# A diffusion block on one core: the modulation product in unsplit float32, in four column groups

## The chip, the core and the metric

The kernel runs on one core of a Trainium2 chip. Its time is the device time of one execution in microseconds (us). Five engines run side by side, each through its own instructions in order: TensorE (PE in the profile; PEld is its weight load), VectorE (DVE), ScalarE (ACT), GpSimd (POOL) and SyncE (SP), whose queue issues nearly all transfers from memory (HBM) to the on-chip buffer. TensorE multiplies a stationary operand, held in its 128 x 128 array, by a moving operand of up to 512 columns, and writes into one of eight banks.

## The reference, cut to what matters

One layer over 256 latent tokens (x) and 256 context tokens (ctx) of width 2048, all in float32. Its first step is the modulation:

```
mod   = silu(c)     @ w_mod + b_mod      # shift, scale, gate of the mixer, then of the MLP
mod_c = silu(c_ctx) @ w_mod + b_mod
hc = rms_norm(ctx) * g * (1 + scale_c) + shift_c
h  = rms_norm(x)   * g * (1 + scale)   + shift
```

`w_mod` is 2048 x 12288. For the mixer both vectors need its first 4096 columns, a shift and a scale for each of the 2048 channels; these are the tensor `wm0` of the kernel, 64 tiles of 128 x 1024 (512 KB each). Then come the input projection `h @ w_in` (its first part, the values, for both token streams), a gated linear recurrence and a convolution, two output projections, and a squared-ReLU MLP. The rest of the layer isn't touched by the change.

## The kernel before

A float32 weight tile is loaded by SP into one of five `raw` buffers, split into a rounded part (`whi`, ACT, line 84) and a remainder (`wlo`, DVE, line 85), both in the format float32r, and multiplied part by part. `Stream` does this in the order of a list (`items`), up to `AHEAD` = 4 tiles ahead of the use. SP waits for a `raw` buffer until DVE has read it.

The stage that the change touches is the first one. It has eight column blocks c, each of 256 channels; a block has eight steps t, one `wm0` tile each. A tile holds two k blocks of 128 rows side by side, each 512 columns wide (256 of the scale, 256 of the shift). In a step, lines 490 and 491 multiply each k block twice, once by `whi` and once by `wlo`; the stationary operand `s4` has four columns, silu(c) and silu(c_ctx), each split in two. So a block is 32 matmuls into four rows of one bank. Then `modulate(c, ps)` runs spread over steps 1 to 3 of the next block: the four rows are copied (line 453), turned into columns by four transposes on PE (line 457), the halves are added and the bias and the gain worked in (lines 466 to 469), which gives `A` and `B` for two channel blocks. `turn` (line 747 and on) then transposes the normed x and ctx for these two channel blocks (eight transposes), applies `A` and `B` on ACT and splits the result into `h` (line 185).

Between the steps, at the places in `STEPS`, half a tile of the values is worked off (`values`, lines 852 to 854): 12 matmuls of 512 columns against a tile of `w_in` (`wi0`, one load and one split for two halves). So a block from c = 2 on has 32 + 24 matmuls of 512 columns, eight transposes of x and ctx, four of `row`, and nine tiles to load and to split.

`norms` loads x and ctx in 8 tiles, in turn with the first weight tiles, sums their squares on ACT and scales them on DVE. After the stage, the rest of the values, the query and the recurrence follow; their tiles (and those of `dots` and `gemv`, which work the other parts of `w_mod` on DVE) come through the same list. [...]

Of the kernel before, what the change touches and what calls it, by code (L numbers as in the profile page):

```python
# [15 lines left out]
P = 128  # L16
# [19 lines left out]
STEPS = [(c, t) for c in range(1, 8) for t in (4, 7)][1:]  # L36
# [12 lines left out]
class Stream:  # L49
# [11 lines left out]

    def add_gemv(self, ap, fn):
        self.items.append((ap, fn, False))

    def prepare(self):
# [4 lines left out]
        raw = kn.wp.tile([P, TW], F32, name="raw", tag="raw", bufs=5)  # L70
        self.dma = nc.sync.dma_start(raw, ap)
        if fn is not None:
            fn(raw)
            return
# [13 lines left out]
    def next(self, ahead=AHEAD):  # L88
        while len(self.ready) < ahead and self.done < len(self.items):
            self.prepare()  # L90
        while ahead > 1 and self.done < len(self.items) and self.items[self.done][1] is not None:
            self.prepare()
        return self.ready.popleft()


class Kernel:
# [190 lines left out]
    def run(self):  # L287
# [18 lines left out]

        cc = pack[:, 0:32]
# [4 lines left out]
        s4 = self.cp.tile([P, KT * 4], F32R, name="s4")  # L312
        s4v = s4.rearrange("p (k f) -> p f k", f=4)
        for i in range(2):
            self.split(sc[:, i * 16:(i + 1) * 16], s4v[:, 2 * i, :], s4v[:, 2 * i + 1, :])
# [23 lines left out]
        for c in range(8):  # L339
            for t in range(8):  # L340
                steps.append((c, t))
                st.add(a["wm0"][8 * c + t])
                if (c, t) in STEPS:
                    steps.append(None)
                    if n % 2 == 0:
                        st.add(a["wi0"][n // 2], paged=True)
                    n += 1
# [68 lines left out]

        def norms():
            ssq = self.cp.tile([P, 8], F32, name="ssq0")
            junk = self.page(F32, "junk")[:, :TW]
            with self.tc.issue_after(exp.ins):  # L420
                nc.scalar.activation(out=first, in_=self.eps, func=AF.Sqrt)
            for n in range(10):
                if n < 8:
                    i, tb, h = n // 4, n // 2 % 2, n % 2
                    nc.sync.dma_start(xt[i][2 * tb + h][:, :TW], a[("x", "ctx")[i]][tb * P:(tb + 1) * P, h * TW:(h + 1) * TW])
                if n > 1:
                    m = n - 2
                    nc.scalar.activation(out=junk, in_=xt[m // 4][m % 4][:, :TW], func=AF.Square, accum_out=ssq[:, m:m + 1])
                if n in (2, 5, 7):
                    yield  # L430
            nc.vector.tensor_reduce(r4, ssq.rearrange("p (t n) -> p t n", n=2), axis=mybir.AxisListType.X, op=ALU.add)
            self.rstd(r4, r4, 1.0 / D)
            for h in range(2):
                for n in range(4):
                    s = xt[n // 2][2 * (n % 2) + h][:, :TW]
                    nc.vector.tensor_scalar(out=s, in0=s, scalar1=r4[:, n:n + 1], scalar2=None, op0=ALU.mult)
                    yield
# [12 lines left out]
        def modulate(c, ps):  # L450

            row = self.small(512, "row")[0:4, :]
            nc.scalar.copy(out=row, in_=ps[0:4, :])
            yield
            pt = self.bank()
            for j in range(4):
                nc.tensor.transpose(out=pt[:, 4 * j:4 * j + 4], in_=row[:, j * P:(j + 1) * P], identity=v["ident"][0:4, 0:4])
            yield

            cols = self.small(16, "cols").rearrange("p (n b i f) -> p n i b f", n=2, b=2, i=2)  # L460
            nc.scalar.copy(out=cols.rearrange("p n i b f -> p n b i f"), in_=pt[:, :16].rearrange("p (n b i f) -> p n b i f", n=2, b=2, i=2))
            ks = slice(2 * c, 2 * c + 2)
            for n, dst in enumerate((Av, Bv)):
                bm = v["bmod"][:, (1 - n) * KT + 2 * c:(1 - n) * KT + 2 * c + 2]
                for i in range(2):
                    nc.vector.tensor_tensor(dst[:, i, ks], cols[:, n, i, :, 0], cols[:, n, i, :, 1], op=ALU.add)
                    nc.vector.tensor_tensor(dst[:, i, ks], dst[:, i, ks], bm, op=ALU.add)
                    if n == 0:
                        nc.vector.scalar_tensor_tensor(dst[:, i, ks], dst[:, i, ks], 1.0, v["g_pm"][:, ks], op0=ALU.add, op1=ALU.mult)
# [5 lines left out]
        for step in steps:  # L475
# [6 lines left out]
            next(normed, None)  # L482
            if t in (1, 2, 3):
                next(late, None)
            hi, lo = st.next()
            for k2 in range(2):
                k = 2 * t + k2
                s = slice(k2 * 512, (k2 + 1) * 512)
                w = s4[:, 4 * k:4 * k + 4]
                nc.tensor.matmul(ps[0:4, :], w, hi[:, s], start=(k == 0), stop=False)  # L490
                nc.tensor.matmul(ps[0:4, :], w, lo[:, s], start=False, stop=(k == KT - 1))  # L491
# [3 lines left out]
        next(values)  # L495
        for _ in late:
            pass
        masks = self.cp.tile([P, 7 * P], U8, name="masks")
# [269 lines left out]
    def warm(self):  # L768

        ps = self.bank()  # L770
        for _ in range(WARM):
# [361 lines left out]
```

## Time and profile before

| | us |
|---|---|
| median of three runs | 1707.87 |
| lowest, highest | 1705.53, 1710.20 |
| the profiled execution, and its span | 1710.28, 1708.5 |
| PE busy in the span | 1665.9 (98%) |
| DVE, ACT busy | 1207.6 (71%), 871.0 (51%) |

The profile records one execution. A matmul's length in it is modelled, from its start to its drained end, so neighbours overlap: what one costs is the distance from its start to the next one's. "Idle before" is the time an engine stood still ahead of a group, with the instruction that ended it. The granted clock is a share of 2.4 GHz, 0.50 being 1.2 GHz.

### The profile page before, as it was taken

What the parts mean: (1) busy time and instruction counts of PE and PEld (TensorE: products, weight loads), DVE (VectorE), ACT (ScalarE), POOL (GpSimd) and SP (SyncE); (2) the same over time, 40 slices, a digit from 0 to 9 for tenths busy, and PEclk for the clock granted to TensorE, in tenths of its full rate; (3) what the DMA queues carried; (4) which work ended last, traced back from release to release, by engine and by line L of the source; (5) the groups of instructions that cost most, each with busy time, mean ns of one, the idle gap of its engine ahead of it and who ended that gap; (6) DMA issues with size and microseconds to landing.
All of it is one profiled execution on the core that took longest, in us unless ns stands there. A gap on an engine that the chain in (4) does not pass through costs nothing.

```text
span 1708.5 us, 23461 instructions
## 1 busy us (share of the span) xinstructions
PE 1665.9 (98%) x8794; PEld 1396.2 (82%) x8794; DVE 1207.6 (71%) x1720; ACT 871.0 (51%) x1268; POOL 8.1 (0%) x18
## 2 busy tenths in 40 slices
PE   5999999999999999999999999999999999999997
PEld 1557887888888888888888899888888888888886
DVE  6887767777776999987897566555665665556555
ACT  8785333344445444564455466445553455345543
POOL 0000000000000000000000000000000000000000
PEclk8999999999999999999999999999999999999999
DMA  9887984433356677668887556666666666666553
GB/s 329 303 303 283 338 283 155 143 125 109 111 162 202 205 236 235 220 202 272 292 273 258 168 198 224 214 228 234 220 208 224 231 227 209 230 222 199 185 188 122
DMA packets 103346, 374.57 MB, mean 219 GB/s; under 512 B 11584, under 2 KB 11584, under 8 KB 103232
## 3 DMA queue, kind: packets, MB, share of 16 engines
q1 hardware_dynamic: 101952, 368.86, 65.0%
q0 software_dynamic: 1280, 4.21, 0.8%
q8 instruction: 69, 1.13, 0.3%
q14 instruction: 45, 0.37, 0.1%
HBM read 370.93 MB, written 2.10 MB: 218 GB/s over the span
## 4 chain that ended last, share of the span: by engine, by line
PE 88%; DVE 4%; DMA 3%; ACT 3%; issue 2%; SPq 0%; DVEq 0%; ACTq 0%
PE bank L200 27%; PE bank L202 14%; PE bank L208 8%; PE bank L209 8%; PE bank L207 8%; PE bank L192 4%; PE bank L190 4%; PE bank L191 4%; DMA raw<-wm 2%; PE bank L910 2%; DVE wlo L85 2%; PE bank L852 1%; PE bank L854 1%; PE bank L853 1%; ACT turned L764 1%
## 5 line engine op out<-in xcount | busy, mean ns | idle before, releaser
L85 DVE TENSOR_TENSOR wlo<-raw,whi 128x1024 fp32r<-128x1024 f32 x547 | 665.5, 1223 | 329.4 <-ACT whi L84 322.9
L84 ACT ACTIVATE whi<-raw 128x1024 fp32r<-128x1024 f32 x547 | 575.6, 1059 | 573.6 <-PE bank L200 204.2
L200 PE MATMUL bank<-h,whi 128*128 128x512 f32 x2176 | 548.3, 394 | 0.0
L200 PEld LDWEIGHTS bank<-h,whi 128*128 128x128 f32 x2176 | 392.7, 189 | 70.6
L202 PEld LDWEIGHTS bank<-h,wlo 128*128 128x128 f32 x2176 | 296.7, 190 | 22.6 <-DVE wlo L85 1.3
L202 PE MATMUL bank<-h,wlo 128*128 128x256 f32 x2176 | 303.6, 282 | 0.5 <-DVE wlo L85 0.4
L207 PE MATMUL bank<-whi,hidh 128*128 128x512 f32 x500 | 194.6, 389 | 0.0
L208 PE MATMUL bank<-wlo,hidh 128*128 128x512 f32 x500 | 194.6, 389 | 0.0
L209 PE MATMUL bank<-whi,hidl 128*128 128x512 f32 x500 | 194.5, 389 | 0.0
L190 PE MATMUL bank<-h,whi 128*128 128x512 f32 (+1 forms) x384 | 140.7, 367 | 1.8 <-ACT whi L84 1.0
L191 PE MATMUL bank<-h,whi 128*128 128x512 f32 (+1 forms) x384 | 136.0, 355 | 0.0
L192 PE MATMUL bank<-h,wlo 128*128 128x512 f32 (+1 forms) x384 | 135.8, 355 | 0.0
L209 PEld LDWEIGHTS bank<-whi,hidl 128*128 128x128 f32 x500 | 93.8, 188 | 19.5
L207 PEld LDWEIGHTS bank<-whi,hidh 128*128 128x128 f32 x500 | 93.9, 188 | 19.4
L208 PEld LDWEIGHTS bank<-wlo,hidh 128*128 128x128 f32 x500 | 93.9, 188 | 19.3
L784 DVE SCALAR_TENSOR_TENSOR gacc<-raw,silu_c,gacc 128x1024 f32<-128x1024 f32 x60 | 76.9, 1282 | 44.3 <-DMA raw<-wm 44.3
L795 DVE SCALAR_TENSOR_TENSOR raw<-raw,silu_row 128x1024 f32<-128x1024 f32 x64 | 77.5, 1221 | 22.9 <-DMA raw<-wmt 22.8
L190 PEld LDWEIGHTS bank<-h,whi 128*128 128x128 f32 x384 | 72.7, 189 | 10.6 <-ACT whi L84 1.2
L192 PEld LDWEIGHTS bank<-h,wlo 128*128 128x128 f32 x384 | 72.3, 189 | 10.5 <-DVE wlo L85 0.3
L191 PEld LDWEIGHTS bank<-h,whi 128*128 128x128 f32 x384 | 72.8, 190 | 8.7 <-DVE h L185 0.3
L490 PE MATMUL bank<-whi,s 128*4 128x512 f32 x128 | 54.2, 423 | 16.6 <-ACT whi L84 16.6
L491 PE MATMUL bank<-wlo,s 128*4 128x512 f32 x128 | 53.8, 420 | 8.4 <-DVE wlo L85 7.9
(206 smaller groups left out, 1514.3 us busy)
## 6 DMA issues: line engine op xcount, KB each, us to landing
raw<-w SPq DMA_DIRECT2D x256, 512.0 KB, 4.2
raw<-wi SPq DMA_DIRECT2D x176, 512.0 KB, 4.2
raw<-wm SPq DMA_DIRECT2D x128, 512.0 KB, 4.6
raw<-wmt SPq DMA_DIRECT2D x64, 512.0 KB, 4.3
raw<-wo SPq DMA_DIRECT2D x32, 512.0 KB, 4.7
raw<-who SPq DMA_DIRECT2D x16, 512.0 KB, 4.4
raw<-wpw SPq DMA_DIRECT2D x16, 512.0 KB, 4.9
x<-x SPq DMA_DIRECT2D x4, 512.0 KB, 7.0
```

The source lines that it names most:

```text
L84: nc.scalar.activation(out=hi, in_=raw, func=AF.Copy)
L85: kn.los.append(nc.vector.tensor_tensor(lo, raw, hi.bitcast(F32), op=ALU.subtract))
L190: nc.tensor.matmul(out, w[0], x[0], start=first, stop=False)
L191: nc.tensor.matmul(out, w[0], x[1], start=False, stop=False)
L192: nc.tensor.matmul(out, w[1], x[0], start=False, stop=last)
L200: nc.tensor.matmul(bank, w[0][:, cut(i)], x(k)[2], start=(k == 0), stop=False)
L202: nc.tensor.matmul(bank[:, T:], w[1][:, cut(i)], x(k)[0], start=False, stop=(k == nk - 1))
L207: nc.tensor.matmul(out, x[0], w[0], start=first, stop=False)
L208: nc.tensor.matmul(out, x[0], w[1], start=False, stop=False)
L209: nc.tensor.matmul(out, x[1], w[0], start=False, stop=last)
L784: nc.vector.scalar_tensor_tensor(acc, raw, s, acc, op0=ALU.mult, op1=ALU.add)
L795: nc.vector.scalar_tensor_tensor(raw, raw, 1.0, self.srow, op0=ALU.mult, op1=ALU.mult, accum_out=self.dot[:, 32 * j + b:32 * j + b + 1])
```

## The change

The 64 `wm0` tiles are no longer split. `add_whole` loads them as they are, the odd steps' tiles into pages of a second pool, up to seven tiles ahead. The stationary operand `s32` holds 32 columns for each k block in plain float32, two of them silu(c) and silu(c_ctx), 30 of them zero. One matmul of line 503 takes the place of two: k block k is written to the 32 rows from 32 * (k % 4) on, that is, through column group k % 4 of the array. A block is 16 matmuls, four to each group. `modulate` copies all 128 rows, transposes 128 x 128 four times (line 470), and one reduction on DVE adds the four groups; fewer, wider instructions make `A` and `B`. x is loaded first, then ctx in turn with weight tiles; x and ctx are normed apart. PE does 32 matmuls of ones ahead of the first step and eight after each of the first four steps. The half tiles of the values go to steps 5 and 7 (before: 4 and 7), and their tiles are split into the ordinary `whi` and `wlo` buffers.

On PE before, around the transposes of x and ctx in the block c = 2 (L490 and L491 are the products with `whi` and `wlo`, L747 the transposes):

```order
L491 MATMUL bank_561<-wlo_534,s4_85 4x512
L490 MATMUL bank_561<-whi_533,s4_85 4x512
L491 MATMUL bank_561<-wlo_534,s4_85 4x512
L490 MATMUL bank_561<-whi_545,s4_85 4x512
L491 MATMUL bank_561<-wlo_546,s4_85 4x512
L490 MATMUL bank_561<-whi_545,s4_85 4x512
L491 MATMUL bank_561<-wlo_546,s4_85 4x512
L747 MATMUL bank_609<-pack_70,x0_102 128x128 x2
L747 MATMUL bank_609<-pack_70,x2_104 128x128 x2
L747 MATMUL bank_621<-pack_70,x0_106 128x128 x2
L747 MATMUL bank_621<-pack_70,x2_108 128x128 x2
```

On PE after the change, block c = 3 from its first step to the values (L503 the unsplit product, L470 the transposes of `row`, L761 those of x and ctx, L866 the values):

```order
L503 MATMUL bank_480<-raw_408,s32_82 32x512 x2
L470 MATMUL bank_489<-pack_70,row_466 128x128 x4
L503 MATMUL bank_480<-rawpage_436,s32_82 32x512 x2
L503 MATMUL bank_480<-raw_440,s32_82 32x512 x2
L503 MATMUL bank_480<-rawpage_456,s32_82 32x512 x2
L761 MATMUL bank_511<-pack_70,x0_100 128x128 x2
L761 MATMUL bank_511<-pack_70,x2_102 128x128 x2
L761 MATMUL bank_523<-pack_70,x0_104 128x128 x2
L761 MATMUL bank_523<-pack_70,x2_106 128x128 x2
L503 MATMUL bank_480<-raw_458,s32_82 32x512 x2
L503 MATMUL bank_480<-rawpage_462,s32_82 32x512 x2
L866 MATMUL bank_341<-whi_483,h4_112 128x512
```

The products of the same tile stand next to each other, and there are half as many; tiles in `raw` and `rawpage` alternate. The run of products without another kind of matmul between is 2, then 6, then 4 long here. Behind these rows the block's last four products follow, between values, in runs of 1 and 3.

On SP before, from the first load of x:

```order
L425 DMA x0_102<-x 128x1024
L425 DMA x1_103<-x 128x1024
L425 DMA x2_104<-x 128x1024
L71 DMA raw_138<-wm0 128x1024
L71 DMA raw_144<-wm0 128x1024
L71 DMA raw_150<-wm0 128x1024
L71 DMA raw_156<-wm0 128x1024
L425 DMA x3_105<-x 128x1024
L425 DMA x0_106<-ctx 128x1024
L425 DMA x1_107<-ctx 128x1024
L71 DMA raw_172<-wm0 128x1024
L425 DMA x2_108<-ctx 128x1024
```

On SP after the change, the same place:

```order
L432 DMA x0_100<-x 128x1024
L432 DMA x1_101<-x 128x1024
L432 DMA x2_102<-x 128x1024
L432 DMA x3_103<-x 128x1024
L432 DMA x0_104<-ctx 128x1024
L78 DMA raw_133<-wm0 128x1024
L432 DMA x1_105<-ctx 128x1024
L78 DMA rawpage_136<-wm0 128x1024
L432 DMA x2_106<-ctx 128x1024
L78 DMA raw_139<-wm0 128x1024
L432 DMA x3_107<-ctx 128x1024
L78 DMA rawpage_142<-wm0 128x1024
```

Four weight tiles stood ahead of the last tile of x and of ctx; now x is whole before the first weight tile, and each further tile of ctx is followed by one of the weights.

```
--- before.py
+++ after.py
@@ -33,7 +33,7 @@
 WARM = 50
 PB = 4
 LIVE = 3
-STEPS = [(c, t) for c in range(1, 8) for t in (4, 7)][1:]
+STEPS = [(c, t) for c in range(1, 8) for t in (5, 7)]
 
 _PACK = [("c", 16), ("cc", 16), ("bmod", 96), ("g_pm", 16), ("g_pl", 16),
          ("dww", 8 * CW), ("dwb", 8), ("lng", 8), ("lnb", 8), ("lbl", 32), ("hng", 8), ("ident", 128)]
@@ -59,6 +59,10 @@
     def add(self, ap, paged=False):
         self.items.append((ap, None, paged))
 
+    def add_whole(self, ap, paged=False):
+
+        self.items.append((ap, "whole", paged))
+
     def add_gemv(self, ap, fn):
         self.items.append((ap, fn, False))
 
@@ -67,8 +71,14 @@
         self.done += 1
         kn = self.kn
         nc = kn.nc
-        raw = kn.wp.tile([P, TW], F32, name="raw", tag="raw", bufs=5)
+        if fn == "whole" and paged:
+            raw = kn.page(F32, "rawpage")[:, :TW]
+        else:
+            raw = kn.wp.tile([P, TW], F32, name="raw", tag="raw", bufs=5)
         self.dma = nc.sync.dma_start(raw, ap)
+        if fn == "whole":
+            self.ready.append(raw)
+            return
         if fn is not None:
             fn(raw)
             return
@@ -88,7 +98,7 @@
     def next(self, ahead=AHEAD):
         while len(self.ready) < ahead and self.done < len(self.items):
             self.prepare()
-        while ahead > 1 and self.done < len(self.items) and self.items[self.done][1] is not None:
+        while ahead > 1 and self.done < len(self.items) and callable(self.items[self.done][1]):
             self.prepare()
         return self.ready.popleft()
 
@@ -304,15 +314,15 @@
         self.dot = self.cp.tile([P, 64], F32, name="dot")
 
 
+        s32 = self.page(F32, "s32")[:, :KT * 32]
+        nc.vector.memset(s32, 0.0)
         cc = pack[:, 0:32]
         sc = self.cp.tile([P, 32], F32, name="silu_c")
         nc.scalar.activation(out=sc, in_=cc, func=AF.Sigmoid)
         nc.vector.tensor_tensor(sc, sc, cc, op=ALU.mult)
         self.sc = sc
-        s4 = self.cp.tile([P, KT * 4], F32R, name="s4")
-        s4v = s4.rearrange("p (k f) -> p f k", f=4)
-        for i in range(2):
-            self.split(sc[:, i * 16:(i + 1) * 16], s4v[:, 2 * i, :], s4v[:, 2 * i + 1, :])
+
+        nc.vector.tensor_copy(s32.rearrange("p (k f) -> p f k", f=32)[:, 0:2, :], sc.rearrange("p (i k) -> p i k", i=2))
 
 
         lbl = v["lbl"].rearrange("p (d l h) -> p d l h", d=2, l=2)
@@ -339,11 +349,11 @@
         for c in range(8):
             for t in range(8):
                 steps.append((c, t))
-                st.add(a["wm0"][8 * c + t])
+                st.add_whole(a["wm0"][8 * c + t], paged=t % 2 == 1)
                 if (c, t) in STEPS:
                     steps.append(None)
                     if n % 2 == 0:
-                        st.add(a["wi0"][n // 2], paged=True)
+                        st.add(a["wi0"][n // 2])
                     n += 1
         for j in range((n + 1) // 2, 8):
             st.add(a["wi0"][j])
@@ -414,27 +424,30 @@
         r4 = self.cp.tile([P, 4], F32, name="r4")
         first = self.cp.tile([P, 1], F32, name="first")
 
+        ssq0 = self.cp.tile([P, 8], F32, name="ssq0")
+        with self.tc.issue_after(exp.ins):
+            nc.scalar.activation(out=first, in_=self.eps, func=AF.Sqrt)
+        for i in range(2):
+            for n in range(4):
+                nc.sync.dma_start(xt[i][n][:, :TW], a[("x", "ctx")[i]][n // 2 * P:(n // 2 + 1) * P, n % 2 * TW:(n % 2 + 1) * TW])
+                if i == 1:
+                    st.prepare()
+        self.warm(32)
+
         def norms():
-            ssq = self.cp.tile([P, 8], F32, name="ssq0")
-            junk = self.page(F32, "junk")[:, :TW]
-            with self.tc.issue_after(exp.ins):
-                nc.scalar.activation(out=first, in_=self.eps, func=AF.Sqrt)
-            for n in range(10):
-                if n < 8:
-                    i, tb, h = n // 4, n // 2 % 2, n % 2
-                    nc.sync.dma_start(xt[i][2 * tb + h][:, :TW], a[("x", "ctx")[i]][tb * P:(tb + 1) * P, h * TW:(h + 1) * TW])
-                if n > 1:
-                    m = n - 2
-                    nc.scalar.activation(out=junk, in_=xt[m // 4][m % 4][:, :TW], func=AF.Square, accum_out=ssq[:, m:m + 1])
-                if n in (2, 5, 7):
-                    yield
-            nc.vector.tensor_reduce(r4, ssq.rearrange("p (t n) -> p t n", n=2), axis=mybir.AxisListType.X, op=ALU.add)
-            self.rstd(r4, r4, 1.0 / D)
-            for h in range(2):
+            for i in range(2):
+                junk = self.page(F32, "junk")[:, :TW]
                 for n in range(4):
-                    s = xt[n // 2][2 * (n % 2) + h][:, :TW]
-                    nc.vector.tensor_scalar(out=s, in0=s, scalar1=r4[:, n:n + 1], scalar2=None, op0=ALU.mult)
-                    yield
+                    m = 4 * i + n
+                    nc.scalar.activation(out=junk, in_=xt[i][n][:, :TW], func=AF.Square, accum_out=ssq0[:, m:m + 1])
+                r = r4[:, 2 * i:2 * i + 2]
+                nc.vector.tensor_reduce(r, ssq0[:, 4 * i:4 * i + 4].rearrange("p (t n) -> p t n", n=2), axis=mybir.AxisListType.X, op=ALU.add)
+                self.rstd(r, r, 1.0 / D)
+                for h in range(2):
+                    for tb in range(2):
+                        x = xt[i][2 * tb + h][:, :TW]
+                        nc.vector.tensor_scalar(out=x, in0=x, scalar1=r[:, tb:tb + 1], scalar2=None, op0=ALU.mult)
+                yield
 
 
         def hx(i):
@@ -449,24 +462,24 @@
 
         def modulate(c, ps):
 
-            row = self.small(512, "row")[0:4, :]
-            nc.scalar.copy(out=row, in_=ps[0:4, :])
+            row = self.small(512, "row")
+            nc.scalar.copy(out=row, in_=ps)
             yield
             pt = self.bank()
             for j in range(4):
-                nc.tensor.transpose(out=pt[:, 4 * j:4 * j + 4], in_=row[:, j * P:(j + 1) * P], identity=v["ident"][0:4, 0:4])
+                nc.tensor.transpose(out=pt[:, j * P:(j + 1) * P], in_=row[:, j * P:(j + 1) * P], identity=v["ident"])
             yield
 
-            cols = self.small(16, "cols").rearrange("p (n b i f) -> p n i b f", n=2, b=2, i=2)
-            nc.scalar.copy(out=cols.rearrange("p n i b f -> p n b i f"), in_=pt[:, :16].rearrange("p (n b i f) -> p n b i f", n=2, b=2, i=2))
+            cols = self.small(8, "cols")
+            nc.vector.tensor_reduce(cols.rearrange("p (j i) -> p j i", i=2), pt.rearrange("p (j g f) -> p j f g", j=4, g=4)[:, :, 0:2, :],
+                                    axis=mybir.AxisListType.X, op=ALU.add)
+            both = lambda w: w.rearrange("p (o k) -> p o k", o=1).broadcast_to([P, 2, 2])
             ks = slice(2 * c, 2 * c + 2)
             for n, dst in enumerate((Av, Bv)):
-                bm = v["bmod"][:, (1 - n) * KT + 2 * c:(1 - n) * KT + 2 * c + 2]
-                for i in range(2):
-                    nc.vector.tensor_tensor(dst[:, i, ks], cols[:, n, i, :, 0], cols[:, n, i, :, 1], op=ALU.add)
-                    nc.vector.tensor_tensor(dst[:, i, ks], dst[:, i, ks], bm, op=ALU.add)
-                    if n == 0:
-                        nc.vector.scalar_tensor_tensor(dst[:, i, ks], dst[:, i, ks], 1.0, v["g_pm"][:, ks], op0=ALU.add, op1=ALU.mult)
+                o = (1 - n) * KT + 2 * c
+                nc.vector.tensor_tensor(dst[:, :, ks], cols[:, 4 * n:4 * n + 4].rearrange("p (b i) -> p i b", i=2), both(v["bmod"][:, o:o + 2]), op=ALU.add)
+                if n == 0:
+                    nc.vector.scalar_tensor_tensor(dst[:, :, ks], dst[:, :, ks], 1.0, both(v["g_pm"][:, ks]), op0=ALU.add, op1=ALU.mult)
             yield
             next(turn)
 
@@ -479,22 +492,23 @@
             c, t = step
             if t == 0:
                 ps = self.bank()
-            next(normed, None)
-            if t in (1, 2, 3):
+            if (c, t) in ((0, 0), (0, 1)):
+                next(normed)
+            if t in (1, 3, 4):
                 next(late, None)
-            hi, lo = st.next()
+            w = st.next(7)
             for k2 in range(2):
                 k = 2 * t + k2
-                s = slice(k2 * 512, (k2 + 1) * 512)
-                w = s4[:, 4 * k:4 * k + 4]
-                nc.tensor.matmul(ps[0:4, :], w, hi[:, s], start=(k == 0), stop=False)
-                nc.tensor.matmul(ps[0:4, :], w, lo[:, s], start=False, stop=(k == KT - 1))
+                g = 32 * (k % 4)
+                nc.tensor.matmul(ps[g:g + 32, :], s32[:, 32 * k:32 * k + 32], w[:, k2 * 512:(k2 + 1) * 512], start=(k < 4), stop=(k >= KT - 4))
+            if c == 0 and t < 4:
+                self.warm(8)
             if t == 7:
                 late = modulate(c, ps)
                 next(late)
-        next(values)
         for _ in late:
             pass
+        next(normed, None)
         masks = self.cp.tile([P, 7 * P], U8, name="masks")
         mi = self.page(I32, "masks_in")[:, :7 * P]
         with self.tc.issue_after(st.dma.ins):
@@ -765,10 +779,10 @@
                     self.turned = self.split(t[:, s], hp[i][k + j][:, :T], hp[i][k + j][:, T:])
             yield
 
-    def warm(self):
+    def warm(self, n=WARM):
 
         ps = self.bank()
-        for _ in range(WARM):
+        for _ in range(n):
             self.nc.tensor.matmul(ps[:, :P], self.ones_r, self.ones_r, start=True, stop=True)
 
     def gemv(self, raw, i, k, h):

```

## Rows read from the trace of the kernel before

**Rows 1.** Stretches: length, busy us (xcount) by engine, granted clock, DMA share, GB/s.
```profile
0.00:32.70 32.70, 14.30 (x36) 3.48 (x36) 16.50 (x30) 27.06 (x39) 0.20 (x4) 0.84 0.92 337
...
50.90:143.40 92.50, 89.37 (x420) 51.01 (x420) 77.29 (x139) 75.46 (x114) 0.00 (x0) 1.00 0.89 308
143.40:240.00 96.60, 96.60 (x491) 82.03 (x491) 71.97 (x109) 40.11 (x56) 0.00 (x0) 1.00 0.86 305
```

**Rows 2.** Timeline of PE: transposes, and twelve matmuls of values.
```profile
53.05 1.03 PE L747 MATMUL bank<-pack,x 128*128 128x128 f32 x8
53.84 0.47 PE L490 MATMUL bank<-whi,s 128*4 128x512 f32 x1
...
55.77 0.40 PE L852 MATMUL bank<-wpage,h 128*128 128x512 f32 x1
...
58.50 0.40 PE L490 MATMUL bank<-whi,s 128*4 128x512 f32 x1
```

**Rows 3.** Timeline of PE: start, length, what; transposes of three blocks' rows.
```profile
32.71 0.41 PE L457 MATMUL bank<-pack,row 4*128 4x4 f32 x4
...
50.86 0.41 PE L457 MATMUL bank<-pack,row 4*128 4x4 f32 x4
...
143.21 0.41 PE L457 MATMUL bank<-pack,row 4*128 4x4 f32 x4
```

**Rows 4.** Groups of instructions, 51 to 143.4 us: busy us, mean ns, idle before.
```profile
L85 DVE TENSOR_TENSOR wlo<-raw,whi 128x1024 fp32r<-128x1024 f32 x49 | 59.1, 1223 | 15.9 <-ACT whi L84 15.6
L84 ACT ACTIVATE whi<-raw 128x1024 fp32r<-128x1024 f32 x48 | 49.9, 1058 | 10.0 <-DMA raw<-wm 7.0 <-DMA raw<-wi 1.2 <-DVE B L466 0.9
L490 PE MATMUL bank<-whi,s 128*4 128x512 f32 x94 | 37.5, 398 | 0.0
L491 PE MATMUL bank<-wlo,s 128*4 128x512 f32 x94 | 37.0, 394 | 3.1 <-DVE wlo L85 2.8
```

**Rows 5.** Waits of the DMA queue, 50.9 to 143.4 us: total, times, longest.
```profile
SPq L71 <- DVE wlo L85: 33.7, 29, 2.7
SPq L71 <- DVE h L185: 16.1, 8, 3.2
```

**Rows 6.** Chain of waits, 60 to 120 us: start, length, what.
```profile
104.67 1.24 DVE wlo L85
105.92 5.00 DMA raw<-wm
```

**Rows 7.** Transfers, 0 to 145 us: issues with KB each and us to landing.
```profile
raw<-wm SPq DMA_DIRECT2D x64, 512.0 KB, 5.3
raw<-wi SPq DMA_DIRECT2D x12, 512.0 KB, 4.6
...
pack<-pack SPq DMA_DIRECT2D x1, 300.0 KB, 2.9
```

**Rows 8.** Transfers, 10 to 25 us: rate, and issues with us to landing.
```profile
DMA packets 1704, 6.20 MB, mean 413 GB/s; under 512 B 191, under 2 KB 191, under 8 KB 1704
...
raw<-wm SPq DMA_DIRECT2D x6, 512.0 KB, 10.2
```

**Rows 9.** Timeline of PE: the unsplit float32 matmuls of 256 columns.
```profile
716.50 1.03 PE L1018 MATMUL bank<-lnred,mean 128*128 128x256 f32 x4
717.36 0.60 PE L978 MATMUL bank<-pack,o 128*128 128x128 f32 x4
```

**Rows 10.** Busy time by stretch at the start.
```profile
0.00:10.00 10.00, 0.00 (x0) 0.00 (x0) 1.93 (x13) 8.76 (x15) 0.20 (x4) 1.00 0.81 261
...
20.00:30.00 10.00, 5.42 (x12) 1.21 (x13) 6.97 (x10) 8.67 (x11) 0.00 (x0) 0.56 0.91 352
```

**Rows 11.** Timeline of PE at the start: first matmul, and two neighbours.
```profile
12.20 0.59 PE L490 MATMUL bank<-whi,s 128*4 128x512 f32 x1 [12.20 <-ACT whi L84]
...
16.83 0.63 PE L491 MATMUL bank<-wlo,s 128*4 128x512 f32 x1
17.26 0.63 PE L490 MATMUL bank<-whi,s 128*4 128x512 f32 x1
```

## The prediction

> **What bounds the kernel now.** I read the busy time by stretch first. From 143.4 us on PE has no idle time (96.60 of 96.60 us in [rows 1]), so a stage that ends earlier there lets all that follows start earlier by as much. Ahead of that point lies the stage that the change touches. PE is at 97% there too (89.37 of 92.50 us in [rows 1]), but matmul lengths overlap, so this doesn't say that it is full; spacing does. Twelve matmuls of 512 columns take 58.50 - 55.77 = 2.73 us, 0.2275 each, and eight transposes 53.84 - 53.05 = 0.79 us [rows 2]. A block needs (32 + 24) x 0.2275 = 12.74, 0.79 and about 0.4 for four transposes, 13.9 us. The timeline shows that it takes (143.21 - 50.86) / 6 = 15.4 us [rows 3]. So 1.5 us a block are waits.
>
> What ends them is in the groups and in the chain. A split costs ACT 1.06 and DVE 1.22 us a tile; DVE waits for ACT 15.6 us in the stretch, ACT for tiles 7.0 us, PE for wlo 2.8 us [rows 4]. SP in turn waits for DVE to release a buffer, 33.7 us for wlo alone [rows 5], and the chain goes round this ring: a split by DVE, then a tile that could only be asked for then, 5.00 us [rows 6]. PE work, split and loads are all near 14 to 15 us a block.
>
> **The change, part by part.** I follow the transposes that close the last block, at 143.21 us before [rows 3]. PE has the same work behind them in both versions, so the time at which they come gives the result.
>
> *Split and ring.* Eight of nine splits a block go: 8 x 1.22 = 9.8 us of DVE and 8 x 1.06 = 8.5 us of ACT [rows 4]. Neither can bind any more. What stays are the loads. A block moves 9 x 0.524 = 4.72 MB [rows 7]. With many transfers queued the rate was 413 GB/s [rows 8], in the stage 308 [rows 1]. So loads need 11.4 us a block at best, and 15.3 if nothing got better. A buffer now comes free when PE has read it, and seven tiles may be under way, so I take the neighbourhood of the best: no bound as long as PE needs over 12 us.
>
> *The unsplit matmul.* The trace has no matmul in a column group, but has float32 ones over the whole array: two matmuls of 256 columns are recorded as four and take 717.36 - 716.50 = 0.86 us [rows 9], 0.215 per recorded pass. That is two passes a matmul, and twice the columns make 0.43 a pass, 0.86 for a matmul of 512 columns, by this rate. The pair that it replaces took 2 x 0.2275 = 0.455. So a block's 16 products cost 16 x 0.86 = 13.8 us if groups don't overlap, against 7.3 before. If four groups run at once, a run of products costs 0.86 for each four begun: runs of 2, 6, 4, 1 and 3, as the order of the change shows, make (1 + 2 + 1 + 1 + 1) x 0.86 = 5.2 us. The other PE work is 24 x 0.2275 = 5.46, 0.79 and 4 x 0.1 = 0.4, together 6.65 us. So a block needs 11.8 us with full overlap and 20.4 without.
>
> Between a run and the other matmuls the array changes its form ten times a block. No row shows what that costs. Bounds: nothing, and one drain each, the recorded length less the spacing, 0.39 - 0.23 = 0.16 us [rows 2, 4], 1.6 us a block; I take half, 0.8. Waits stay too: the values need the h of the transposes three steps before and the split of their tile. Between none and the 1.5 us of before I take 1.1, since the product that covered the way is shorter now. That is 11.8 + 0.8 + 1.1 = 13.7 us a block.
>
> The Trainium skill (TensorE: Matmul & The Clock Gate, "Measured speedup vs the span model") gives 2.38 times for three column groups of 512 columns, nearly full overlap; no run here shows it yet. By that factor alone the 13.8 us would come to 5.8, and the sum would move by 0.6 us a block.
>
> *The first block.* Its end is set by loads: pack (0.3 MB), eight tiles of x and ctx and eight of weights, 8.7 MB [rows 7]. The first 10 us moved 2.6 MB [rows 10], the rest takes 6.1 / 0.413 = 14.8 us, so the last tile lands at about 25 and the block closes at 27, against 32.71 [rows 3]: 5.7 us won. Before, the fifth tile sat behind x and ctx in the queue and PE stood still with its clock down, 0.56 in 20 to 30 us [rows 10]. The added matmuls of ones fill time in which PE waits for a tile (its first product began at 12.20 us, [rows 11]); without that cover they cost 32 + 32 times about 0.1 us, 0.8 of every 6.4 us a group of eight.
>
> *The rest of the edits.* Copy, wider transposes and one reduction in place of two rounds of small adds lie on ACT and DVE, which have the 8 to 10 us a block to hide them; the values one step later cost nothing by themselves. Below nothing I see no gain there, above it at most the 1.5 us a block of waits counted already.
>
> *Sum.* 27 + 7 x 13.7 = 123 us against 143.2: 20 us off. The profiled execution took 1710.28, which gives 1690. The median of the runs is 2.4 us lower, so 1688 in their terms. Seven blocks at 12 to 15 us (loads at their best with no change of form, and all drains with the old waits) give a range of 1676 to 1699 for this case.
>
> **The rivals.** *Only neighbours overlap.* The two passes of one matmul use the same group, so the second can't run beside the first. If PE starts matmuls strictly in order, the next group's first pass waits until that second pass starts, and each matmul adds one pass: a run of n costs (n + 1) x 0.43, here (3 + 7 + 5 + 2 + 4) x 0.43 = 9.0 us. A block is then 9.0 + 6.65 + 1.1 = 16.8 us, and 27 + 7 x 16.8 = 144.6, so about 1709, the first block's gain spent. For it speaks that each float32 matmul is two records [rows 9]; against it, that nothing here shows how passes queue. The Trainium skill has that rule in the same page ("The mechanism"): matmuls begin and end in program order.
>
> *No overlap.* PE works the groups one after another, since all of them stream through the same rows. A block is 13.8 + 6.65 + 1.1 = 21.5 us, 27 + 7 x 21.5 = 177.5, 34 us more than before: 1742. It is slower from 15.4 - 6.65 - 1.1 = 7.65 us for the 16 products on, 0.48 each. For it: the only float32 rate in the trace is 0.86. Against it: only that the groups use separate columns.
>
> *A lower clock.* PE waits for tiles in the first block, and rows show the clock down there (0.56, [rows 10]) with products 17.26 - 16.83 = 0.43 apart [rows 11] where 0.23 is the full rate. If waiting between tiles kept PE at 1.2 GHz in the later blocks, 11.8 us of PE work would be 23.6 and the time about 1755. Against it: with 11.8 of 13.7 us worked there is little waiting, and from 50.9 on the clock was 1.00 with 1.5 us of waits a block [rows 1].
>
> **How the numbers follow.** Full overlap has 0.56, neighbours only 0.22, no overlap 0.15, and the clock 0.07, of which little ends below today's time. A measurement of this kernel tells about 0.3% (5.1 us) from no change. Full overlap is faster; of the second case about a quarter is faster, half the same and a quarter slower; the last two are slower but for 0.02. That makes faster 0.63, same 0.12, slower 0.25. The range goes from 1675 to 1718: it holds the first case and the second with its drains and leaves out the last two and small ends.
>
> **What would show it right or wrong.** In the changed kernel's timeline the spacing of L503 decides: four starts within 0.86 us are full overlap, 0.43 apart is neighbours only, 0.86 apart none. The transposes of `row` should close blocks every 13.7 us, first at 27 and last near 123. SP should wait for PE, not for DVE, and the rate should be 345 GB/s (4.72 MB in 13.7 us). DVE should lose some 9 us of busy time a block. I am wrong if L503 starts 0.48 us apart or more on the average, or if the clock in 50 to 120 us is below 1.

## The result, and the profile after

The changed kernel takes 1716.76 us, the median of 9 runs (1711.62 to 1723.43). The kernel before takes 1708.85 in the 9 runs beside it (1705.53 to 1710.74). The ratio is 1.0050 with a 95% interval of 1.0033 to 1.0067: slower by half a per cent, where I had forecast 1688 and faster. The changed kernel's runs also spread more, over 11.8 us against 5.2.

The profiled execution took 1719.32 us with a span of 1717.5. In its timeline of PE the transposes of `row` (line 470, 457 before) close the blocks at these times; columns are start, length, what it is, and in brackets the idle time before it with its releaser:

```profile
31.36 0.66 PE L470 MATMUL bank<-pack,row 128*128 128x128 f32 x4 [0.68 <-ACT row L466]
45.91 0.66 PE L470 MATMUL bank<-pack,row 128*128 128x128 f32 x4
62.94 0.66 PE L470 MATMUL bank<-pack,row 128*128 128x128 f32 x4
...
130.93 0.66 PE L470 MATMUL bank<-pack,row 128*128 128x128 f32 x4
151.28 0.66 PE L470 MATMUL bank<-pack,row 128*128 128x128 f32 x4 [4.28 <-ACT row L466]
```

Against [rows 3] the first block closes 1.35 us earlier and the second 4.95 us earlier. Then the lead goes: the next five blocks take 17.0 us each, and the last one 20.35, where the six took 15.4 on the average. The last closes 151.28 - 143.21 = 8.1 us later than before. Behind it the kernel is what it was: 1566.2 us of the span are left there, and 1565.3 were left before. So nearly the whole loss arises ahead of 151 us. (The two profiled executions lie 9.0 us apart, the medians 7.9.)

The busy time by stretch (length, busy us and instructions of PE, PEld, DVE, ACT and POOL, granted clock, DMA share, GB/s) answers to [rows 1]:

```profile
0.00:31.30 31.30, 24.14 (x100) 15.45 (x100) 8.39 (x25) 16.13 (x27) 0.20 (x4) 1.00 0.95 366
45.90:151.20 105.30, 90.05 (x406) 43.79 (x404) 24.84 (x60) 34.30 (x67) 0.00 (x0) 0.90 0.75 271
```

DVE and ACT are relieved as the change promises: DVE has 24.84 us of work in six blocks where it had 77.29, ACT 34.30 where it had 75.46. But PE now stands idle for 15.25 of 105.30 us, where it stood for 3.1 of 92.50, its granted clock is 0.90 where it was 1.00, and the loads move 271 GB/s where they moved 308. The queue of the loads (line 78) waits for PE now, as the waits of SP from 45.9 to 143 us show (total, times, longest):

```profile
SPq L78 <- PE bank L503: 61.2, 23, 5.2
SPq L78 <- DVE h L195: 15.5, 6, 3.0
```

In [rows 5] it waited for DVE. So the loads no longer wait for splits but for PE, and PE waits for no load in these blocks.

One block, in the timeline of PE, shows what does:

```profile
46.49 0.62 PE L503 MATMUL bank<-rawpage,s 128*32 128x512 f32 x2
46.51 0.62 PE L503 MATMUL bank<-raw,s 128*32 128x512 f32 x2
46.95 0.60 PE L503 MATMUL bank<-rawpage,s 128*32 128x512 f32 x2
46.96 0.60 PE L503 MATMUL bank<-raw,s 128*32 128x512 f32 x2
47.38 1.03 PE L503 MATMUL bank<-rawpage,s 128*32 128x512 f32 x4
48.33 1.09 PE L761 MATMUL bank<-pack,x 128*128 128x128 f32 x8
...
49.82 0.60 PE L503 MATMUL bank<-rawpage,s 128*32 128x512 f32 x2
52.27 0.73 PE L866 MATMUL bank<-whi,h 128*128 128x512 f32 x2 [1.84 <-ACT whi L94]
52.93 1.72 PE L503 MATMUL bank<-raw,s 128*32 128x512 f32 x2
54.58 0.80 PE L867 MATMUL bank<-wlo,h 128*128 128x512 f32 x1
55.18 0.63 PE L868 MATMUL bank<-whi,h 128*128 128x512 f32 x1
55.60 0.63 PE L867 MATMUL bank<-wlo,h 128*128 128x512 f32 x1
...
57.22 0.40 PE L866 MATMUL bank<-whi,h 128*128 128x512 f32 x1
57.45 0.39 PE L867 MATMUL bank<-wlo,h 128*128 128x512 f32 x1
```

The first rows answer what the forecast turned on. Four passes start within 0.02 us of each other (46.49 and 46.51), the next four 0.45 later: four column groups do run at once. Then PE stops for some 2 us before the first matmul of the values, which waits for the split of its tile (`whi`, line 94); 1.84 us of that are recorded as idle. Behind this stop the two passes of one product take 1.65 us (52.93 to 54.58), where e2 below has 0.95, and the values start 0.43 apart instead of 0.23. That is half speed, and the granted clock says so:

```profile
45.90:50.30 4.40, 4.40 (x34) 1.82 (x32) 0.56 (x4) 1.27 (x3) 0.00 (x0) 1.00 1.01 379
50.30:52.30 2.00, 0.15 (x5) 0.04 (x1) 0.48 (x2) 2.00 (x5) 0.00 (x0) 1.00 0.85 299
52.30:54.60 2.30, 2.30 (x5) 0.42 (x5) 2.18 (x4) 0.83 (x3) 0.00 (x0) 0.69 1.02 392
54.60:56.50 1.90, 1.90 (x6) 1.52 (x6) 0.00 (x0) 0.00 (x0) 0.00 (x0) 0.50 1.01 408
56.50:62.90 6.40, 6.40 (x29) 3.43 (x27) 0.00 (x0) 0.59 (x1) 0.00 (x0) 0.99 0.60 227
```

Read the columns of PE and ACT side by side: from 50.3 to 52.3 us PE works 0.15 us and ACT all 2.00. The clock goes to 0.50 (1.2 of 2.4 GHz) after the stop and is back at 56.5.

What ACT does there is in its own timeline:

```profile
49.03 1.94 ACT L778 ACTIVATE turned<-bank,B,A 128x256 f32<-128x256 f32 x4 [6.31 <-PE bank L761]
50.84 0.43 ACT L195 ACTIVATE h<-turned 128x256 fp32r<-128x256 f32 x1
51.15 1.07 ACT L94 ACTIVATE whi<-raw 128x1024 fp32r<-128x1024 f32 x1
52.09 1.04 ACT L195 ACTIVATE h<-turned 128x256 fp32r<-128x256 f32 x3
```

ACT stood idle for 6.31 us until PE's transposes came, then made four `turned` and one `h`, and only then the split. That is the order in which the program lists ACT's instructions: the split stands behind most of the turn.

The last block has a stop of its own, 4.28 us before the row of 151.28 above. ACT's timeline there:

```profile
147.03 1.06 ACT L94 ACTIVATE whi<-raw 128x1024 fp32r<-128x1024 f32 x1 [6.04 <-PE bank L868]
148.10 1.28 ACT L824 ACT_TABLE_LOAD   x1
149.60 1.15 ACT L824 ACTIVATE sig<-silu_row 128x512 f32<-128x512 f32 x2 [0.21 <-DMA silu_row<-crow]
150.66 0.57 ACT L466 COPY row<-bank 128x512 f32<-128x512 f32 x1
```

The copy of the last row (line 466), for which PE's transposes wait, stands behind a split, a table load and the sigmoid of the next stage (line 824), which waits for a load of its own.

### The profile page after: what moved, and what is told of

It is laid out like the page before. It is cut to its first block, busy times and chain, and to the rows that moved or that the text cites. A ratio compares the mean times of both kernels' runs of the same rounds, so it can differ in the third digit from the quotient of the medians.

```text
span 1717.5 us, 23270 instructions
## 1 busy us (share of the span) xinstructions
PE 1676.7 (98%) x8858; PEld 1401.0 (82%) x8858; DVE 1131.8 (66%) x1610; ACT 807.3 (47%) x1195; POOL 8.1 (0%) x18
## 4 chain that ended last, share of the span: by engine, by line
PE 90%; ACT 3%; DMA 3%; DVE 3%; issue 1%; SPq 0%; DVEq 0%; ACTq 0%
PE bank L210 26%; PE bank L212 14%; PE bank L219 8%; PE bank L218 8%; PE bank L217 8%; PE bank L202 4%; PE bank L200 4%; PE bank L201 4%; PE bank L503 3%; DMA raw<-wm 2%; PE bank L924 2%; PE bank L867 2%; PE bank L866 2%; PE bank L868 2%; ACT turned L778 1%; ACT whi L94 1%
## 5 line engine op out<-in xcount | busy, mean ns | idle before, releaser
L95 DVE TENSOR_TENSOR wlo<-raw,whi 128x1024 fp32r<-128x1024 f32 x490 | 597.0, 1223 | 313.9 <-ACT whi L94 307.6
L94 ACT ACTIVATE whi<-raw 128x1024 fp32r<-128x1024 f32 x490 | 516.4, 1059 | 561.7 <-PE bank L210 200.5
L866 PE MATMUL bank<-whi,h 128*128 128x512 f32 x128 | 51.9, 417 | 12.0 <-ACT whi L94 12.0
L867 PE MATMUL bank<-wlo,h 128*128 128x512 f32 x128 | 54.6, 427 | 0.0
```

The costliest lines, as they stand in the source:

```text
L94: nc.scalar.activation(out=hi, in_=raw, func=AF.Copy)
L95: kn.los.append(nc.vector.tensor_tensor(lo, raw, hi.bitcast(F32), op=ALU.subtract))
L866: nc.tensor.matmul(o, xh[:, ts_], hi[:, s], start=(k == 0), stop=False)
L867: nc.tensor.matmul(o, xh[:, ts_], lo[:, s], start=False, stop=False)
```

## The experiments

Three theories. *Wait*: PE stops because ACT's list puts the split (and, in the last block, the next stage's sigmoid) ahead of what PE needs, and the stop takes the clock along. *Groups*: products in column groups pull the clock down by themselves, and the wait is a side effect. *Loads*: with the stop gone, transfers would end each block no earlier. Each run's time is compared with the kernel before on the same chip (median 1708.42 for e1, e2, e4 and e5, 1708.79 for the others); intervals are 95%.

**e1_fill: matmuls of ones into the stop.**

```diff
             if c == 0 and t < 4:
                 self.warm(8)
+            if c > 1 and t == 5:
+                self.warm(18)
```

> The changed kernel, with 18 matmuls of ones behind the products of step 5 in the blocks from c = 2 on, where PE stands still 2.0 us before the values. Theory W (the products overlap as meant; a block of 17.0 us loses 2.0 us to the wait for the split that ACT runs behind the turn, and about 2.0 us to the lower clock that follows the wait): the wait is filled and still ends at the same instruction, the 2.0 us of slow matmuls go, blocks of about 15.0 us, and some 10 to 12 us less in all: about 1705. Theory G (the products in column groups pull the clock down themselves, not the idle time): matmuls behind the first half tile of values are still 0.43 us apart, blocks stay at 17.0, time as the changed kernel or a little above, 1717 to 1720.

Measured: 1710.53 us (1707.36 to 1711.22), ratio 1.0009 (1.0000 to 1.0018). Timeline of PE:

```profile
53.16 1.67 PE L788 MATMUL bank<-ones_r 128*128 128x128 f32 x13
54.66 1.13 PE L868 MATMUL bank<-whi,h 128*128 128x512 f32 x4
55.63 0.39 PE L869 MATMUL bank<-wlo,h 128*128 128x512 f32 x1
55.86 0.40 PE L870 MATMUL bank<-whi,h 128*128 128x512 f32 x1
...
62.48 0.66 PE L470 MATMUL bank<-pack,row 128*128 128x128 f32 x4
```

The values run 0.23 apart at once, and a block takes 62.48 - 47.09 = 15.4 us instead of 17.0. Keeping PE at work with nothing useful is worth 1.6 us a block, nearly all of it clock. (The ones also part the run of four products in two, and the lone product joins the next run; by the spacing these cost and save about 1 us.) *Groups* falls, since as many products run in groups as before at a clock of 1.00. The gain is smaller than I expected because ones fill slightly more than the stop, the first block closed 1.2 us later in this run (32.54), and the last block still has its stop (4.08 us). Between the profiled executions it is 9.4 us, between the medians 6.2: the changed kernel's profiled execution lies 2.6 us above its median.

**e2_split_first: the split ahead of the turn on ACT.** In the loader the split's instruction is kept, and the turn's instructions are issued behind it.

```diff
-            nc.scalar.activation(out=hi, in_=raw, func=AF.Copy)
+            self.cut = nc.scalar.activation(out=hi, in_=raw, func=AF.Copy)
...
-            next(turn)
+            with ExitStack() as after:
+                if c < 7:
+                    after.enter_context(self.tc.issue_after(st.cut.ins))
+                next(turn)
```

> The changed kernel, with the split of the values' tile ahead of the turn's instructions on ACT instead of behind them; nothing else on PE is added or left out. Theory W: the 2.0 us wait before the values falls below 0.5 us and the clock stays up, blocks from c = 2 to 6 take 13.0 to 13.5 us instead of 17.0, so 17 to 20 us less than the changed kernel: 1697 to 1700, and faster than the kernel before by about 10. Theory L (loads bind: 4.72 MB a block at the 270 to 290 GB/s of the stage): the wait moves to the tiles, blocks stay above 16 us, 1712 or more. Theory G: the clock falls all the same, about 15 us a block, 1707.

Measured: 1695.27 us (1693.59 to 1696.37), ratio 0.9922 (0.9908 to 0.9936). ACT's timeline in the same block:

```profile
46.76 1.06 ACT L94 ACTIVATE whi<-raw 128x1024 fp32r<-128x1024 f32 x1 [4.37 <-DMA raw<-wi]
48.70 1.02 ACT L781 ACTIVATE turned<-bank,B,A 128x256 f32<-128x256 f32 x2 [0.89 <-PE bank L764]
```

and PE's, with the start of the block, and from the one product of its own to the end:

```profile
45.58 0.66 PE L470 MATMUL bank<-pack,row 128*128 128x128 f32 x4
...
49.92 1.02 PE L506 MATMUL bank<-raw,s 128*32 128x512 f32 x2
50.87 0.50 PE L869 MATMUL bank<-whi,h 128*128 128x512 f32 x1
...
58.76 0.66 PE L470 MATMUL bank<-pack,row 128*128 128x128 f32 x4
```

The split now runs when its tile has landed, in time in which ACT was idle anyway. A block takes 58.76 - 45.58 = 13.17 us, without a stop and at a clock of 1.00. The same work in the same groups; one instruction elsewhere in ACT's list turns half a per cent lost into 0.8 won, a little more than I expected. PE's list changed at one place with it: the lone product now stands ahead of the first two values and not behind them, so a block changes form eight times instead of ten. By the second block of the changed kernel, which has no slow clock, that is worth about 0.2 us. In the last block PE still stops, 1.24 us before the values and 3.50 before the row. *Wait* stands. *Loads* falls: between 45.6 and 111.4 us they move 364 GB/s and PE never waits.

**e4_tail: four tiles ahead instead of seven in the last block**, so that the next stage's load and sigmoid are not drawn ahead of the last copy of `row`.

```diff
-            w = st.next(7)
+            w = st.next(7 if c < 7 else 4)
```

> The changed kernel, looking ahead 4 tiles instead of 7 in the last block alone, which puts the last block's row copy on ACT ahead of the sigmoid that waits for the row of c. Theory W: PE's 4.3 us of standing still at the last block's transposes go, and the slow restart behind it (about 1 us); blocks before stay at 17.0 us: about 1712. If the row copy is late for another reason than its place on ACT, the wait stays and so does the time, 1717.

Measured: 1712.80 us (1707.50 to 1714.95), ratio 1.0022 (1.0011 to 1.0033), as expected. The blocks still take 17.0 us; the last takes 16.7 and closes at 147.24:

```profile
137.77 2.07 PE L866 MATMUL bank<-whi,h 128*128 128x512 f32 x4 [2.75 <-ACT whi L94]
...
147.24 0.60 PE L470 MATMUL bank<-pack,row 128*128 128x128 f32 x4
```

Its row is there without a stop, and no slow start follows. The stop before the values is still there, and longer in this block (2.75 us), since ACT's list now has the split behind the whole turn. So the second fault costs 4 us of the 8, 4.8 if it is taken from e2 to e6, and its remedy works without the first one's.

**e6_both: e2 and e4 together.**

> The changed kernel with both earlier edits: the split of the values' tile ahead of the turn on ACT, and four tiles ahead in the last block. Theory W: the two gains are of different places and add up, 1695.3 less the 3.5 us wait at the last transposes and about 1.5 us of its slow restart: about 1690 (1688 to 1692), a ratio of 0.989 to 0.991 to the kernel before. If the waits only trade places, 1695 as with the first edit alone.

Measured: a median of 1690.51 us, ratio 0.9895 (0.9880 to 0.9911); one of five executions read 3351.86 for a reason that isn't known, and the ratio leaves it out. The stretch from the second block's end to the last's:

```profile
45.90:125.00 79.10, 79.10 (x405) 40.07 (x405) 21.83 (x56) 31.56 (x63) 0.00 (x0) 1.00 0.94 348
```

PE is busy for all of it at a full clock, the loads move 348 GB/s, and the last block closes at 124.94. The two edits give back all that the change had lost and 1% beside: some 26 us against the change as made. The gains add up: 21.5 us by e2 and 4.0 by e4 alone.

**e5_one_group: all products in column group 0**, which takes away the overlap. The copy, transposes and sum are of 32 rows instead of 128.

```diff
-                g = 32 * (k % 4)
+                g = 0
...
-            nc.scalar.copy(out=row, in_=ps)
+            nc.scalar.copy(out=row[0:32, :], in_=ps[0:32, :])
```

> The changed kernel, with all products of a block in column group 0 and 32 rows of one bank, so that no two can run beside each other; the reduction over the groups becomes a copy. Theory W: products start 0.86 us apart, two passes of 0.43 each; the run of six takes 5.2 us instead of 1.84, and a block 22 to 25 us, 45 to 60 us more in all: 1760 to 1775. If the groups gave nothing, no change.

Measured once: 1753.37 us, less than the 1760 that I expected at least. Timeline of PE, a run of products:

```profile
57.87 1.90 PE L502 MATMUL bank<-rawpage,s 128*32 128x512 f32 x4
59.62 1.88 PE L502 MATMUL bank<-raw,s 128*32 128x512 f32 x4
61.33 1.88 PE L502 MATMUL bank<-rawpage,s 128*32 128x512 f32 x4
```

Four passes take 1.71 to 1.75 us, one after another, 0.43 each and 0.86 for a product. A block is 21.5 us at a clock of 1.00, against 13.17 in e2: the four groups are worth 8.3 us a block. Nor is there a stop before the values here, since the longer products cover the split on ACT.

The next three start from e6 and ask what the edits at the start are worth.

**e7_no_ones: no matmuls of ones.**

```diff
-        self.warm(32)
...
-            if c == 0 and t < 4:
-                self.warm(8)
```

> The same with both edits, and without any of the matmuls of ones in the first block. Theory S (the ones of 128 columns do not bring the clock up, and those between the products lie on PE's way): the first block closes no later, or 1 to 2 us earlier than at about 31.5 us, time the same or up to 2 us less than with both edits. Theory H (the ones help the clock): products stay 0.43 us a pass apart longer in the first blocks, 2 to 5 us more.

Measured: 1691.43 us (1689.66 to 1691.84), ratio 0.9898 (0.9884 to 0.9911). Timeline of PE:

```profile
27.85 0.66 PE L469 MATMUL bank<-pack,row 128*128 128x128 f32 x4
...
35.84 1.04 PE L505 MATMUL bank<-raw,s 128*32 128x512 f32 x2 [1.51 <-DMA raw<-wm]
...
44.87 0.66 PE L469 MATMUL bank<-pack,row 128*128 128x128 f32 x4
```

The first block closes 3.4 us earlier than in e6, the second only 0.9 earlier: at 35.84 PE waits for a tile, with loads running at 411 GB/s from 10 to 45 us. The second block is bound by loads.

**e8_wide_ones: the same with ones of 512 columns**, 34 ahead of the first step and 4 behind each of four.

```diff
-        self.warm(32)
+        self.warm_wide(34)
...
-                self.warm(8)
+                self.warm_wide(4)
```

> The same with both edits, and the matmuls of ones made 512 columns wide (34 ahead of the first product, 4 behind each of the first four tiles' products; the scheduler puts 16 of these together behind the first tile, and loads the first weight tile ahead of x). Theory S: wide ones bring the clock up where those of 128 columns did not (they are 0.22 us apart for all 7.1 us of the start, twice the 0.11 of full clock), so the products of the first block are 0.43 us a pass apart and no longer 0.85, and the block closes at about 28 us instead of 31.5: 2 to 4 us less. If the width of the ones makes no difference, no change, or the time of the ones on top.

Measured: 1691.08 us (1689.88 to 1692.57), ratio 0.9898 (0.9885 to 0.9912).

```profile
2.90 9.69 PE L797 MATMUL bank<-ones_w,ones_r 128*128 128x512 f32 x34 [2.90 <-ACT ones_w L308]
12.52 1.05 PE L508 MATMUL bank<-raw,s 128*32 128x512 f32 x4
...
37.01 1.92 PE L508 MATMUL bank<-raw,s 128*32 128x512 f32 x2 [1.51 <-DMA raw<-wm]
```

These ones do bring the clock up: the first two products take 1.05 us, where in the change as made they took 1.92. The first block closes at 28.15, but PE then waits for tiles, and behind the last wait the clock is at 0.50 from 37 to 40 us: the product at 37.01 takes 1.85 us to the next start, where e7 has 1.02. The second block closes at 47.39, 2.5 us later than in e7. No gain either.

**e9_old_order: x, ctx and the first weight tiles loaded in the order of before.** The four weight tiles go behind the third load of x, one more behind the second of ctx.

```diff
-        for i in range(2):
-            for n in range(4):
...
-                if i == 1:
-                    st.prepare()
+        for m in range(8):
+            i, n = m // 4, m % 4
...
+            for _ in range({2: 4, 5: 1}.get(m, 0)):
+                st.prepare()
```

> The same with both edits, and x, ctx and the first weight tiles loaded in the order of the kernel before. Theory: the first product starts 3 to 4 us earlier, but the block needs the same 8.7 MB before its last product, so it closes within 1 us of the same time, and the total is within 2 us. If the new order is what gains in the first block, as forecast (5 us), then 4 to 5 us more.

Measured: 1690.63 us (1689.44 to 1692.42), ratio 0.9896 (0.9883 to 0.9910), the same as e6. The first product starts earlier (11.70 against 13.65 us), the first block closes at 30.71, the second at 46.24. The order of loads gives nothing that can be measured.

## Why the prediction was wrong

**The step that failed is the term for waits, 1.1 us a block**, taken "between none and the 1.5 of before". In five blocks the stop and the half clock behind it cost 17.03 - 13.17 = 3.9 us (e2): 2.0 for the stop, 1.6 for the clock (e1), and about 0.2 for two more changes of form. The last block, with a second stop, took 20.35 - 13.17 = 7.2 more. I had bounded the new kernel's waits by those of the old one, though the old ones had another cause: short waits for a split in a steady ring (2.8 us for `wlo` in the whole stretch, seven times, 0.6 at most). They were also less than 1.5 us a block: the last block before has three half tiles of values and not two, 2.7 us more work, and the other five take 15.1 us each, 1.2 above my sum. The prediction said itself that the values "need the h of the transposes three steps before and the split of their tile" and that "the product that covered the way is shorter now", and then put no row to it. The rows were there. A split takes ACT 1.06 us [rows 4], and before, the values' split stood among eight others, with products on PE's list meanwhile. With eight of nine gone it stands alone, and its place in ACT's list decides: if it is listed behind the turn, the way from PE's transposes at 48.33 is 0.7 us to the first `turned`, four `turned` and one `h` to 51.15, the split to 52.22, and the values start at 52.27. What PE has to do meanwhile is eight transposes and a run of four products, to 50.3. The 2 us are the difference. ACT having 8 us to spare in a block was true and beside the point.

**The last block.** 20.35 us was not foreseen at all. I counted "seven tiles may be under way" only as a help for loads. Looking seven tiles ahead also draws the next stage's work into the last block, and onto the engine that must copy `row`. Its price, 4 to 5 us, is in e4 and e6.

**The lower clock** was a rival with a chance of 0.07, argued away with "there is little waiting". On the share of time that was right, 2 of 17 us; but it is one piece, and behind it the clock was at 0.50 until 56.5. Before, in the stretch from 50.9 us on, no wait was longer than 0.6 us, and the clock stayed at 1.00. The sign that I had named for being wrong, a clock below 1 in 50 to 120 us, came: it was 0.90. The Trainium skill (TensorE: Matmul & The Clock Gate, "HAM oscillation — how this bites in real kernels") tells of a kernel in which a wait for a transfer between tiles brings the clock down again in every tile. The trace agrees, with another wait in that place: for ACT, once in each block, 1.6 us each time.

**What held.** Full overlap: four passes at once, 0.43 a pass. The forecast took 5.2 us a block for products and 11.8 for PE's work; e2 measures 13.17 without waits, which leaves 1.4 us for eight changes of form and whatever else the sum lacks, where I took 0.8 of at most 1.6 for ten. The Trainium skill ("Measured speedup vs the span model", same page) gives 2.38 for three column groups; a run of four products takes 0.89 us in e2 and 3.55 in e5, 4.0 times; no run here has three groups. "Only neighbours overlap" did not come. The Trainium skill has the rule that spoke for it (same page, "The mechanism"): matmuls begin and end in program order. In the rows above the second passes of four products all start together behind their four first ones, so that a later product's first pass begins before an earlier one's second. Whether that goes against the rule is not shown, since no row tells in which order the program lists the passes; for the time of a run, the measurement decides. "No overlap" had 21.5 us a block and 1742; e5 has 21.5 and 1753, and most of the rest is its first block, which closes at 36.02 and not at 27.

DVE lost 8.7 us of work a block (77.29 - 24.84 over six), forecast some 9. SP waits for PE, as said. Loads need not bind: at 345 GB/s, forecast for blocks of 13.7 us, e6 measures 348 with blocks of 13.2.

**The first block** was forecast to close at 27 by loads alone, and does at 27.85 without the ones (e7). With them it closes at 31.36: the ones did not only "fill time in which PE waits". The first thirty-two did (7.09 us, over 4.2 us before the first product), but those between the first steps ran when the products could have: the fourth tile's products begin at 26.59, in e7 at 20.48. It did no harm in the end, because the second block waits for tiles whatever the first does (0.98 us at 36.72 in e6, 1.51 in e7, e8 and e9): e6 and e7 differ by less than their intervals.

**The sum.** With both stops gone, e6 is near the kernel that I forecast: 1690.5 us against 1688, last block closed at 124.94 against 123. That they meet so closely is in part luck: the first block closes 4.2 us later than forecast, and the others have no waits, where I took 1.1, but dearer changes of form. In the range for the first case, 1676 stands in terms of the median and 1699 in those of the profiled execution; both in terms of the median are 1676 and 1697. The range to 1718 held the measured 1716.76, but by the second rival's numbers, not by a wait that I had priced.

## What to carry to other kernels

When a change takes most of one kind of work off an engine, look at what is left of it: where each remaining instruction stands in that engine's list, and what it now stands behind. Spare time on an engine hides an instruction only if the list lets it run in that time. And a stop of 2 us on TensorE is priced with what follows it; here the half clock nearly doubled it.

## What the runs showed of the hardware

Float32 matmuls of 512 columns, each recorded as two passes, run at the same time in four column groups: four passes start within 0.02 us, the next four 0.45 us later. A run of four takes 0.89 us, and 3.55 in one group (e2, e5).

The 32 ones of 128 columns at the start are 0.21 us apart from the first to the last, where e1 has 0.115 at full clock, so they ended with the clock still down; the first two products took 1.92 us with them (e6, and the change as made, 4.2 us after the last of them; e9 after 2.2) and without any (e7). Of the 34 ones of 512 columns in e8 the first eight are 0.43 apart and the others 0.23, and the products that follow at once take 1.05. What a pause behind wide ones would have taken back is not shown.

A stop does not always bring the clock down. Behind that of 1.84 us it went to 0.50 in each of the six blocks. Behind one of 1.51 us it stayed at 1.00 in e7 and e9; in e8, where one of 1.11 us came 2.6 us earlier, it went to 0.50 behind the same 1.51.

In the changed kernel's first 31 us the granted clock reads 1.00 while products take twice their later time (1.92 against 1.05 for two), up to 29.15; the trace's first record of the clock comes at 29.3 us. At the start of this kernel the spacing tells the clock and that column does not.
